# Two decoder layers on one core: the sample group's value products in one PSUM bank with one set of transposes, and the gate's transposes and products in pairs at separate places

## The chip, the cores and the metric

The kernel runs on one core of a Trainium2 chip. The metric is the device time of one execution in microseconds (us), taken as the median of several runs. TensorE is called PE in the profile (PEld is its weight load), VectorE DVE, ScalarE ACT, GpSimd POOL, and SyncE, which issues most transfers, SP.

## The reference, cut to what matters

The program is one inference step of a two-layer decoder. A prompt group of 256 positions and a sample group of 8 sequences, with one new position each and 256 cached ones, share all weights. What the change touches are two things.

The first is the attention of the eight samples over their cached pages, in both layers. A sequence has two pages of 128 positions, 8 heads and 64 columns per head:

```python
# layer 0, softmax; layer 1 has stick-breaking weights in place of p
s = jnp.einsum('hqd,hqjsd->hqjs', qh, ks).astype(jnp.float32) * scale
p = jax.nn.softmax(s.reshape(H, qb, -1), axis=-1).reshape(s.shape)
return jnp.einsum('hqjs,hqjsd->qhd', p.astype(vs.dtype), vs)
```

The second is the spatial gate of layer 0, where each of four groups of 128 channels is mixed over the 128 positions of a chunk by a lower triangular matrix:

```python
w = jnp.tril(sgu_w[:, :c, :c])
vg = v.reshape(B, nc, c, B_GROUPS, B_GROUP_DIM)
f = jnp.einsum('gts,bnsgd->bntgd', w, vg) + sgu_b[:, :c].T[None, None, :, :, None]
return u * f.reshape(B, T, B_WIDTH)
```

## The kernel before

**Layout.** All activations stand transposed: 128 channels of a group on the partitions, the 264 positions (256 of the prompt, then the 8 samples) in the free dimension. So one product with a 128x128 block of weights serves both groups at once.

**Blocks and phases.** `run` (L310) walks through a fixed list of weight blocks per phase: in0, out0, ff0, dn0 for layer 0, and in1, out1, ff1, dn1 for layer 1. A block is three products of 128x264 in one PSUM bank (L329 to L333): high half of the weights by high and by low half of the activations, then low half by high half. Weights come in chunks, are split by ACT (high half, `wh`, L300) and DVE (low half, `wl`, L303) three tiles of eight blocks ahead, in buffers that PE has to free first. in0 has 160 blocks, in1 128; eight blocks in turn make one output `mm`, which DVE then takes out of PSUM. In out0 and out1 the first blocks take `catB` (the gate's or pool mixer's half) in the order of its four parts: block 0 takes part 0, block 2 part 2, block 3 part 3.

**What is put between the blocks.** Everything else that PE does is put between blocks by hand: `blk(b, f)` calls `f` once `b` blocks of the phase have been issued. PE executes in the order written. The times of the calls are the hooks, L925 to L967 for layer 0 and L1126 to L1152 for layer 1.

**PSUM.** Eight banks of 512 fp32 columns: four belong to the pool of `mm` (L228), four to the pool of `at` (L229). `mmb` (L251) borrows a bank from the first pool for other work. A bank is taken again once its reader is done.

**The samples' values.** `sm_tr` (L819) and `zs_tr` (L1066) transpose the weights of all eight sequences, and `to_pz` (L485) copies them into `PZ`, a buffer zeroed once, with 32 columns per page and sequence of which the first eight hold the heads: one ACT instruction per page. `sample_av` (L491) is called for two groups of four sequences: sixteen fp32 products' worth of `pv` into a bank of its own, each sequence in a strip of 32 partitions, then one ACT copy (L498) into `msk`. The calls stand at blocks 157 and 159 of in0 (L957) and 100 and 108 of in1 (L1143). `sample_out` (L503) transposes `msk` back in four 128x128 parts per group, that is eight `po` transposes, and hands out four views, which DVE adds or copies into `osam` (L837, L1076). It is called by `sm_out` at block 4 of out0 and by `zs_out` at block 1 of out1.

**The gate.** `gm_tr(t)` (L887) transposes part t of the normalised `bv` in two 128x128 pieces into a bank `vtp_sgu` of the `mm` pool, and ACT copies it into `vgt` (L522). All four stand at block 150 (L950). `gm_gate(t)` (L896) makes two fp32 products into a bank `pf` of the `mm` pool; DVE adds the bias (L900), multiplies by `bu` (L902), and ACT and DVE make `catB`'s high and low half (L445, L446). All four stand at block 155 (L953). At block 155 of in0 GpSimd also does `gm_own` on the sample columns.

**Stick-breaking around hook 100 of in1.** `z_qk(t)` scores two heads (`Z`, blocks 80, 93, 105, 117); ACT and DVE turn them into weights `w` (sigmoids L1019 and L1020, scan L1021, product L1022); `z_tr(t)` transposes these in 2 x 3 pieces `pt` (blocks 91, 104, 116, and one in out1).

Of the kernel before, what the change touches and what calls it, by code (L numbers as in the profile page):

```python
# [13 lines left out]
AF = mybir.ActivationFunctionType  # L14
# [4 lines left out]
P = 128  # L19
# [3 lines left out]
NS = 8  # L23
T = SEQ + NS
HD = 64
NH = 8
PAST = 256
PAGE = 128
NPG = PAST // PAGE
# [173 lines left out]
def tile_decoder_step(ctx: ExitStack, tc: tile.TileContext, a):  # L203
    nc = tc.nc
    v, s, g = nc.vector, nc.scalar, nc.gpsimd
# [14 lines left out]
    pe = TensorE()  # L220
# [10 lines left out]
    def f4(name, shape=(P, 4, T), dt=F32):  # L231
        return up.tile(list(shape), dt, tag="u", name=name)
# [7 lines left out]
    def at(name):  # L240
        return psa.tile([P, 512], F32, tag="at", name=name)
# [9 lines left out]
    def mmb(name):  # L251

        return psm.tile([P, 512], F32, tag="mm", name=name)
# [5 lines left out]
    def cst(n):  # L259
        o, w = _CST[n]  # L260
        return CST[:, o:o + w]
# [123 lines left out]
    ident = cst("ident")  # L385
# [62 lines left out]
    def page_list(cache, name):  # L448

        tiles, todo = [], []  # L450

        def load(i):
            if i % NPG == 0:
                tiles.append(f4(f"{name}_{i}", (P, NPG, 512)))
            late(tiles[i // NPG][:, i % NPG, :], cache[bass.ds(regs[i], 1), :, :].rearrange("o p f -> (o p) f"))

        return tiles, [lambda i=i: load(i) for i in range(NS * NPG)]
# [27 lines left out]
    def to_pz(src, fn):  # L485

        for pg in range(NPG):
            s.activation(PZ[:, pg, :, 0:NH].rearrange("p s (t c) -> p t s c", c=2),
                         src[:, pg * P:(pg + 1) * P].rearrange("p (t x) -> p t x", x=32)[:, :, :2 * NS].rearrange("p t (s c) -> p t s c", c=2), fn)

    def sample_av(msk, pz, vtiles, gr, name):  # L491
        pv = at(f"pv_{name}{gr}")
        for pg in range(NPG):
            for j in range(4):
                sq = 4 * gr + j
                pe.matmul(pv[32 * j:32 * j + 32, :], pz[:, pg, sq, :], vtiles[sq][:, pg, :],
                          start=pg == 0, stop=pg == NPG - 1)
        s.activation(msk[:, gr], pv, AF.Copy)  # L498

    def sample_av_of(st, pz, vtiles, gr, name):  # L500
        return lambda: sample_av(st["msk"], pz, vtiles, gr, name)

    def sample_out(msk, name):  # L503

        out = []
        for gr in range(2):
            po = at(f"po_{name}{gr}")
            for t in range(4):
                pe.transpose(po[:, 126 * t:126 * t + P], msk[:, gr, t * P:(t + 1) * P], ident)
            for c in range(2):  # L510
                out.append((64 * c, 4 * gr, po[64 * c:64 * c + 64, c::32].rearrange("p (t s) -> p t s", s=4)))
        return out

    PZ = con.tile([P, NPG, NS, 32], F32, name="PZ")
    g.memset(PZ, 0.0)
# [2 lines left out]
    def v_pair(vt, src, t, name, bank=None):  # L518
        p = (bank or at)(f"vtp_{name}{t}")
        for kb in range(2):  # L520
            pe.transpose(p[:, kb * P:(kb + 1) * P], src[:, kb * P:(kb + 1) * P], ident)
        s.activation(vt[:, :, t * P:(t + 1) * P], p[:, :2 * P].rearrange("p (b d) -> p b d", b=2), AF.Copy)  # L522
# [226 lines left out]
    vtiles, vload = page_list(a["vp0"], "V0")  # L749
    st0 = {}  # L750
# [68 lines left out]
    def sm_tr():  # L819
        pr = st0["ps"]  # L820
        pP = mmb("pP")
        for pg in range(NPG):
            pe.transpose(pP[:, pg * P:(pg + 1) * P], pr[:, pg * P:(pg + 1) * P], ident)
        to_pz(pP, AF.Copy)
        pO = mmb("pO")
        pe.matmul(pO[:, :4 * NS], cst("hs"), st0["ow"], start=True, stop=True)
        ob = sm.tile([P, 4, NS], F32, tag="ob", name="ob", bufs=1)
        s.activation(ob, pO[:, :4 * NS].rearrange("p (t s) -> p t s", s=NS), AF.Copy)
        st0["ob"] = ob
        st0["msk"] = f4("msk0", (P, 2, 512))  # L830

    def sm_out():
        osam = sm.tile([P, 4, NS], F32, tag="osam", name="osam", bufs=1)
        v.tensor_tensor(osam, st0["ob"], v4[:, :, SEQ:T], ALU.mult)
        for b, q, po in sample_out(st0["msk"], "l0"):
            o = osam[b:b + 64, :, q:q + 4]
            v.tensor_tensor(o, o, po, ALU.add)  # L837
        halves(catA[0][:, :, SEQ:T], catA[1][:, :, SEQ:T], osam)
# [75 lines left out]
    blk = lambda b, f, *x: hk.at(b / 8 - 1, f, *x)  # L914
# [30 lines left out]
    blk(131, gm_gelu)  # L945
    blk(130, gm_norm)
    blk(140, sm_tr)
    blk(144, lambda: nc.sync.dma_start(a["k0"], k4))
    for t in range(4):
        blk(150, gm_tr, t)  # L950
    blk(155, gm_own)
    for t in range(4):
        blk(155, gm_gate, t)  # L953
    for t, b in enumerate((146, 154, 162)):
        if b <= 160:
            blk(b, lambda t=t: v_pair(vt, v4[:, t, :], t, "v0"))
    for i, b in enumerate((157, 159)):  # L957
        blk(b, sample_av_of(st0, PZ, vtiles, i, "l0"))
# [20 lines left out]
    vtiles, vload = page_list(a["vp1"], "V1")  # L979
# [16 lines left out]
    st1 = {}  # L996
# [69 lines left out]
    def zs_tr():  # L1066
        pP = mmb("pP1")
        for pg in range(NPG):
            pe.transpose(pP[:, pg * P:(pg + 1) * P], st1["zs"][:, pg * P:(pg + 1) * P], ident)
        to_pz(pP, AF.Copy)  # L1070
        st1["msk"] = f4("msk1", (P, 2, 512))

    def zs_out():
        osam = sm.tile([P, 4, NS], F32, tag="osam", name="osam1", bufs=1)
        for b, q, po in sample_out(st1["msk"], "l1"):
            v.tensor_copy(osam[b:b + 64, :, q:q + 4], po)  # L1076
        halves(catA[0][:, :, SEQ:T], catA[1][:, :, SEQ:T], osam)
# [47 lines left out]
    blk = lambda b, f, *x: hk.at(b / 8 - 1, f, *x)  # L1125
    blk(14, norm1)  # L1126
    blk(33, pool_sum)
    for n in range(8):
        blk(40 + 8 * n, drip_of(vload, 2))
    blk(72, zs_score)  # L1130
    blk(82, zs_tr)
    for t, b in enumerate((80, 93, 105, 117)):
        blk(b, z_qk, t)
# [6 lines left out]
        blk(b, pool_mix, i)  # L1140
    for t, b in enumerate((110, 118, 126)):
        blk(b, lambda t=t: v_pair(vt, v4[:, t, :], t, "v1", mmb))
    for i, b in enumerate((100, 108)):  # L1143
        blk(b, sample_av_of(st1, PZ, vtiles, i, "l1"))
    run(orders["in1"], pick(xg), in1_evac, hk)
    hk = Hooks()
# [82 lines left out]
```

## Time and profile before

| What | us |
|---|---|
| median of 3 runs (599.3 to 599.55) | 599.43 |
| the profiled execution | 599.23 |
| its span in the trace | 597.2 |
| PE busy in the span | 588.4 |
| DVE busy in the span | 423.4 |
| ACT busy in the span | 342.5 |
| POOL busy in the span | 104.8 |

The profiled execution is 0.20 us below the median; 2.03 us of it lie outside the span. PE is busy nearly all the time, so whatever it does between the blocks of weights is time of the kernel. A timeline row gives an instruction's start and duration (or those of several alike, with their count), and in brackets how long its engine stood idle before it and what ended that. PE's durations overlap: the next product starts before the last one has ended, so its cost is read from the distance between starts.

### The profile page before, as it was taken

To read this page: it belongs to the slowest core of one execution; us is meant where nothing else is said; L and a number is where in the kernel's file an instruction comes from. 1 tells how busy PE (TensorE), PEld (TensorE's weight loads), DVE (VectorE), ACT (ScalarE), POOL (GpSimd) and SP (SyncE) were. 2 spreads that over 40 slices of the span, in tenths; PEclk is the share of its full clock that TensorE was granted. 3 is DMA by queue.
4 is the path that set the end of the run, shared out by engine and by line. 5 is a ranking of instruction groups with operands and counts; after the bars stand their busy time and mean duration, and the time that the engine had idled before them with its cause. 6 is when DMAs were issued, how large, how long until landed. Compare 5 with 4: busy or idle time off the path is not lost.

```text
span 597.2 us, 12397 instructions
## 1 busy us (share of the span) xinstructions
PE 588.4 (99%) x4907; PEld 570.4 (96%) x4907; DVE 423.4 (71%) x739; ACT 342.5 (57%) x600; POOL 104.8 (18%) x99
## 2 busy tenths in 40 slices
PE   9999999999999999999999999999999999999995
PEld 8999879999999999999999879999999999999994
DVE  7999566877777777655659676687777777864442
ACT  7757845676565655644453556567656565564441
POOL 2100003212313232110120000121232323211110
PEclk9999999999999999999999999999999999999998
DMA  8898844545454545895567763554545454555502
GB/s 334 339 399 348 293 158 156 212 147 204 150 205 153 204 151 202 280 373 201 177 224 278 260 207 97 171 211 148 206 149 206 150 204 156 198 175 198 200 1 74
DMA packets 27707, 122.41 MB, mean 205 GB/s; under 512 B 3330, under 2 KB 4482, under 8 KB 16258
## 3 DMA queue, kind: packets, MB, share of 16 engines
q1 hardware_dynamic: 27072, 120.55, 56.2%
q10 hardware_dynamic: 578, 1.07, 0.5%
q8 instruction: 39, 0.64, 0.4%
q14 instruction: 18, 0.15, 0.1%
HBM read 117.65 MB, written 3.96 MB: 204 GB/s over the span
## 4 chain that ended last, share of the span: by engine, by line
PE 97%; DMA 1%; DVE 1%; ACT 0%; DVEq 0%; issue 0%; SPq 0%
PE mm L215 90%; PE pv_l L215 1%; PE sc L215 1%; PE pav L215 1%; PE pt L218 1%; DMA xw<-in_xw 1%; PE S L215 1%; PE Z L215 1%; PE pf L215 0%; DVE y L643 0%; PE pm L215 0%; PE vtp_v L218 0%; PE po_l L218 0%; PE vtp_sgu L218 0%; PE ns_fin L215 0%; DVE wl L666 0%
## 5 line engine op out<-in xcount | busy, mean ns | idle before, releaser
L303 DVE TENSOR_TENSOR wl<-raw,wh 128x1024 fp32r<-128x1024 f32 x179 | 219.6, 1228 | 74.4 <-ACT wh L300 74.3
L300 ACT ACTIVATE wh<-raw 128x1024 fp32r<-128x1024 f32 x179 | 188.3, 1055 | 90.2 <-PE mm L215 83.3
L215 PE MATMUL mm<-xg_f_h,wh 128*128 128x264 f32 x704 | 200.4, 285 | 0.0
L215 PE MATMUL mm<-xg_f_l,wh 128*128 128x264 f32 x704 | 200.1, 284 | 0.0
L215 PE MATMUL mm<-xg_f_h,wl 128*128 128x264 f32 x704 | 198.9, 283 | 0.0
L215 PEld LDWEIGHTS mm<-xg_f_l,wh 128*128 128x128 f32 x704 | 132.4, 188 | 0.0
L215 PEld LDWEIGHTS mm<-xg_f_h,wh 128*128 128x128 f32 x704 | 132.3, 188 | 0.0
L215 PEld LDWEIGHTS mm<-xg_f_h,wl 128*128 128x128 f32 x704 | 132.3, 188 | 0.0
L585 POOL TENSOR_TENSOR wk<-wk 128x264 f32<-128x264 f32 x44 | 66.2, 1506 | 194.3 <-DVE wk L584 169.0
L215 PE MATMUL mm<-a_h,wh 128*128 128x264 f32 x352 | 100.2, 285 | 0.0
L215 PE MATMUL mm<-a_l,wh 128*128 128x264 f32 x352 | 100.0, 284 | 0.0
L215 PE MATMUL mm<-a_h,wl 128*128 128x264 f32 x352 | 99.5, 283 | 0.0
L215 PEld LDWEIGHTS mm<-a_l,wh 128*128 128x128 f32 x352 | 66.2, 188 | 0.0
L215 PEld LDWEIGHTS mm<-a_h,wh 128*128 128x128 f32 x352 | 66.2, 188 | 0.0
L215 PEld LDWEIGHTS mm<-a_h,wl 128*128 128x128 f32 x352 | 66.1, 188 | 0.0
L445 ACT ACTIVATE a_h<-wk 128x264 fp32r<-128x264 f32 x44 | 18.7, 424 | 73.4 <-POOL wk L585 73.4
L446 DVE TENSOR_TENSOR a_l<-wk,a_h 128x264 fp32r<-128x264 f32 x44 | 19.2, 437 | 41.5 <-ACT a_h L445 41.5
L215 PE MATMUL mm<-xg_h,wh 128*128 128x264 f32 x160 | 47.8, 299 | 0.0
L215 PE MATMUL mm<-xg_h,wl 128*128 128x264 f32 x160 | 45.5, 285 | 0.2 <-DVE wl L666 0.2
L215 PE MATMUL mm<-xg_l,wh 128*128 128x264 f32 x160 | 45.5, 285 | 0.0
L215 PE MATMUL mm<-xg_n_h,wh 128*128 128x264 f32 x128 | 38.5, 301 | 0.0
L215 PE MATMUL mm<-xg_n_l,wh 128*128 128x264 f32 x128 | 36.3, 284 | 0.0
(254 smaller groups left out, 897.7 us busy)
## 6 DMA issues: line engine op xcount, KB each, us to landing
raw<-in_w SPq DMA_DIRECT2D x89, 1024.0 KB, 4.8
K<-in_kt SPq DMA_DIRECT2D x32, 256.0 KB, 6.4
V<-in_vp SPq DMA_DIRECT2D x32, 256.0 KB, 6.9
raw<-in_w SPq DMA_DIRECT2D x4, 512.0 KB, 6.1
X<-in_x SPq DMA_DIRECT2D x4, 264.0 KB, 7.7
xw<-in_xw SPq DMA_DIRECT2D x2, 388.0 KB, 5.4
out_k<-k SPq DMA_DIRECT2D x1, 528.0 KB
out_v<-v SPq DMA_DIRECT2D x1, 528.0 KB, 4.7
```

Of the source, the lines that this page charges most:

```text
L215: return self.keep(nc.tensor.matmul(*x, **k))
L218: return self.keep(nc.tensor.transpose(*x, **k))
L300: i = s.activation(h, src, AF.Copy)
L303: i = v.tensor_tensor(l, src, h.bitcast(F32), ALU.subtract)
L445: s.activation(h, src, AF.Copy)
L446: v.tensor_tensor(l, src, h.bitcast(F32), ALU.subtract)
L585: g.tensor_tensor(A, A, C, ALU.mult)
```

## The change

There are three edits.

1. `to_pz` writes the heads of the second group of sequences into columns 8 to 15 instead of 0 to 7, with one ACT instruction per page and group (four instead of two). `sample_av` makes the products of both groups into one bank `pv`: the second call adds to what the first has left, and a product of one group adds zeros to the rows of the other. The ACT copy into `msk` is made once, after the second call, and `msk` has half the columns. `sample_out` makes four transposes instead of eight; its four views come from one bank. The number of `pv` products stays.
2. The gate's transposes stand at blocks 149, 149, 151 and 151 instead of four times 150; its products at 155, 155, 158 and 158 instead of four times 155. So the second pair of products is issued between the two calls of `sample_av`.
3. In layer 1 `sample_av` stands at blocks 109 and 112 instead of 100 and 108.

```diff
@@ to_pz, sample_av, sample_out
         for pg in range(NPG):
-            s.activation(PZ[:, pg, :, 0:NH].rearrange("p s (t c) -> p t s c", c=2),
-                         src[:, pg * P:(pg + 1) * P].rearrange("p (t x) -> p t x", x=32)[:, :, :2 * NS].rearrange("p t (s c) -> p t s c", c=2), fn)
-
-    def sample_av(msk, pz, vtiles, gr, name):
-        pv = at(f"pv_{name}{gr}")
+            w = src[:, pg * P:(pg + 1) * P].rearrange("p (t x) -> p t x", x=32)[:, :, :2 * NS].rearrange("p t (s c) -> p t s c", c=2)
+            for gr in range(2):
+                s.activation(PZ[:, pg, 4 * gr:4 * gr + 4, gr * NH:gr * NH + NH].rearrange("p s (t c) -> p t s c", c=2), w[:, :, 4 * gr:4 * gr + 4, :], fn)
+
+    def sample_av(st, pz, vtiles, gr, name):
+
+        if gr == 0:
+            st["pv"] = at(f"pv_{name}")
+        pv = st["pv"]
         for pg in range(NPG):
             for j in range(4):
                 sq = 4 * gr + j
                 pe.matmul(pv[32 * j:32 * j + 32, :], pz[:, pg, sq, :], vtiles[sq][:, pg, :],
-                          start=pg == 0, stop=pg == NPG - 1)
-        s.activation(msk[:, gr], pv, AF.Copy)
+                          start=gr == 0 and pg == 0, stop=gr == 1 and pg == NPG - 1, skip_group_check=True)
+        if gr == 1:
+            s.activation(st["msk"], pv, AF.Copy)
 
     def sample_out(msk, name):
 
-        out = []
-        for gr in range(2):
-            po = at(f"po_{name}{gr}")
-            for t in range(4):
-                pe.transpose(po[:, 126 * t:126 * t + P], msk[:, gr, t * P:(t + 1) * P], ident)
-            for c in range(2):
-                out.append((64 * c, 4 * gr, po[64 * c:64 * c + 64, c::32].rearrange("p (t s) -> p t s", s=4)))
-        return out
+        po = at(f"po_{name}")
+        for t in range(4):
+            pe.transpose(po[:, 126 * t:126 * t + P], msk[:, t * P:(t + 1) * P], ident)
+        return [(64 * c, 4 * gr, po[64 * c:64 * c + 64, 8 * gr + c::32].rearrange("p (t s) -> p t s", s=4)) for gr in range(2) for c in range(2)]
@@ layer 0
-        st0["msk"] = f4("msk0", (P, 2, 512))
+        st0["msk"] = f4("msk0", (P, 512))
     for t in range(4):
-        blk(150, gm_tr, t)
+        blk((149, 149, 151, 151)[t], gm_tr, t)
     blk(155, gm_own)
     for t in range(4):
-        blk(155, gm_gate, t)
+        blk((155, 155, 158, 158)[t], gm_gate, t)
@@ layer 1
-        st1["msk"] = f4("msk1", (P, 2, 512))
+        st1["msk"] = f4("msk1", (P, 512))
-    for i, b in enumerate((100, 108)):
+    for i, b in enumerate((109, 112)):
         blk(b, sample_av_of(st1, PZ, vtiles, i, "l1"))
```

More of the change, by code (lines that the diff above doesn't have):

```diff
@@ L496, in sample_av @@
                 pe.matmul(pv[32 * j:32 * j + 32, :], pz[:, pg, sq, :], vtiles[sq][:, pg, :],
-                          start=pg == 0, stop=pg == NPG - 1)
-        s.activation(msk[:, gr], pv, AF.Copy)
+                          start=gr == 0 and pg == 0, stop=gr == 1 and pg == NPG - 1, skip_group_check=True)
+        if gr == 1:
+            s.activation(st["msk"], pv, AF.Copy)
     def sample_av_of(st, pz, vtiles, gr, name):
-        return lambda: sample_av(st["msk"], pz, vtiles, gr, name)
+        return lambda: sample_av(st, pz, vtiles, gr, name)
     def sample_out(msk, name):
-        out = []
-        for gr in range(2):
-            po = at(f"po_{name}{gr}")
-            for t in range(4):
-                pe.transpose(po[:, 126 * t:126 * t + P], msk[:, gr, t * P:(t + 1) * P], ident)
-            for c in range(2):
-                out.append((64 * c, 4 * gr, po[64 * c:64 * c + 64, c::32].rearrange("p (t s) -> p t s", s=4)))
-        return out
+        po = at(f"po_{name}")
+        for t in range(4):
+            pe.transpose(po[:, 126 * t:126 * t + P], msk[:, t * P:(t + 1) * P], ident)
+        return [(64 * c, 4 * gr, po[64 * c:64 * c + 64, 8 * gr + c::32].rearrange("p (t s) -> p t s", s=4)) for gr in range(2) for c in range(2)]
     PZ = con.tile([P, NPG, NS, 32], F32, name="PZ")
```

## The prediction

> **What bounds the kernel now.** I read the page first: busy times, then the chain of work that ended last.
>
> ```profile
> PE 588.4 (99%) x4907; PEld 570.4 (96%) x4907; DVE 423.4 (71%) x739; ACT 342.5 (57%) x600; POOL 104.8 (18%) x99
> PE 97%; DMA 1%; DVE 1%; ACT 0%; DVEq 0%; issue 0%; SPq 0%
> ```
>
> PE is 97% of the chain. So a microsecond that PE doesn't spend between the blocks of weights is one off the time, and what only ACT, DVE or a transfer does counts only where PE would come to wait for it. The next view is PE's timeline where foreign work is put in, because PE's durations overlap and only distances between starts tell a cost.
>
> ```profile
> 72.24 0.28 PE L215 MATMUL mm<-xg_l,wh 128*128 128x264 f32 x1
> 72.36 0.28 PE L215 MATMUL mm<-xg_h,wl 128*128 128x264 f32 x1
> 72.49 0.38 PE L218 MATMUL vtp_v<-CST,v 128*128 128x128 f32 x2
> 72.62 0.37 PE L215 MATMUL mm<-xg_h,wh 128*128 128x264 f32 x1
> 72.83 0.29 PE L215 MATMUL mm<-xg_l,wh 128*128 128x264 f32 x1
> ```
>
> Undisturbed, products start 0.12 us apart (72.24, 72.36), a block of three takes 0.36. The measure that I use throughout is: start of the second product after the insertion, minus start of the last before it, minus the 0.24 that two steps take anyway. Here it gives 72.83 - 72.36 - 0.24 = 0.23 us for two transposes.
>
> **The `po` transposes, halved in both layers.** The eight of layer 0 in the same timeline:
>
> ```profile
> 87.09 0.28 PE L215 MATMUL mm<-catB_h,wl 128*128 128x264 f32 x1
> 87.22 1.03 PE L218 MATMUL po_l<-CST,msk 128*128 128x128 f32 x8
> 88.01 0.37 PE L215 MATMUL mm<-catB_h,wh 128*128 128x264 f32 x1
> 88.21 0.28 PE L215 MATMUL mm<-catB_l,wh 128*128 128x264 f32 x1
> ```
>
> 88.21 - 87.09 - 0.24 = 0.88. From two to eight the cost grows by 0.65, 0.108 per transpose, and at two it is already almost nothing but that: an insertion of transposes has next to no fixed price. Four, which have no row, lie between 0.23 and 0.88; the line through both ends gives 0.45. Saved: 0.43 per layer, **0.86** for two.
>
> **The gate's transposes in two pairs.** Before, all four `vtp_sgu` (eight transposes) stand together:
>
> ```profile
> 74.05 0.28 PE L215 MATMUL mm<-xg_h,wl 128*128 128x264 f32 x1
> 74.17 1.30 PE L218 MATMUL vtp_sgu<-CST,bv 128*128 128x128 f32 x8
> 74.59 1.30 ACT L522 ACTIVATE vgt<-vtp_sgu 128x256 f32<-128x256 f32 x4 [0.34 <-PE vtp_sgu L218]
> 75.03 0.20 PEld L218 LDWEIGHTS vtp_sgu<-CST,bv 128*128 128x128 f32 x2 [0.28 <-ACT vgt L522]
> 75.22 0.37 PE L215 MATMUL mm<-xg_h,wh 128*128 128x264 f32 x1
> ...
> 75.43 0.28 PE L215 MATMUL mm<-xg_l,wh 128*128 128x264 f32 x1
> ```
>
> They cost 75.43 - 74.05 - 0.24 = 1.14, where eight `po` cost 0.88. The row at 75.03 says why: of the four `mm` banks the running output holds one, so the fourth pair waits for ACT's first copy. Two insertions of four cost 2 x 0.45 = 0.90. Saved: **0.24**, if the second pair finds its bank free.
>
> **The gate's products in two pairs.** Sixteen records (each fp32 product leaves two):
>
> ```profile
> 77.23 0.28 PE L215 MATMUL mm<-xg_h,wl 128*128 128x264 f32 x1
> 77.23 1.43 PEld L215 LDWEIGHTS pf<-sguc,vgt 128*128 128x128 f32 x12
> ...
> 78.83 0.52 PEld L215 LDWEIGHTS pf<-sguc,vgt 128*128 128x128 f32 x4 [0.17 <-DVE bv L900]
> ...
> 79.50 0.28 PE L215 MATMUL mm<-xg_l,wh 128*128 128x264 f32 x1
> ```
>
> Cost: 79.50 - 77.23 - 0.24 = 2.03. The first twelve loads take 1.43, the last of them 0.19 itself, so they come 0.113 apart; the twelfth starts at 78.47, the thirteenth at 78.83 instead of 78.58, because its bank had to be read by DVE first. That is 0.25 of standing. Eight records have no row: without a fixed price they cost 8 x 0.113 = 0.90, two insertions 1.80, and 0.23 is saved. The other end is that a separate insertion costs as much again as the standing, which saves nothing. I take **0.23**, since the nearest row, the two transposes in the same 128*128 shape, shows no fixed price.
>
> **The `pv` products.** Their number stays. In layer 1 they move:
>
> ```profile
> 349.97 0.28 PE L215 MATMUL mm<-xg_n_h,wl 128*128 128x264 f32 x1
> 350.18 1.92 PE L215 MATMUL pv_l<-V,PZ 128*32 128x512 f32 x16
> 352.03 0.39 PE L215 MATMUL mm<-xg_n_h,wh 128*128 128x264 f32 x1
> 352.26 0.28 PE L215 MATMUL mm<-xg_n_l,wh 128*128 128x264 f32 x1
> ```
>
> A call costs 352.26 - 349.97 - 0.24 = 2.05 wherever it stands. Half of its products add to an open bank already (the second page), so adding in the second call is nothing new. Cost: 0.
>
> **What becomes late.** With the call at hook 100 gone, PE comes to the transposes of hook 104 earlier: 349.97 plus four blocks (1.45) is 351.42. The second three of them, 0.33 later at 351.75, need the stick-breaking product of the fourth head:
>
> ```profile
> 350.90 0.55 DVE L1022 TENSOR_TENSOR w<-w,keep 128x384 f32<-128x384 f32 x1
> ```
>
> It is done at 351.45, and all that it hangs on lies ahead of hook 100, so it doesn't move. 0.3 us remain, a call's 2.05 less than before. After that, PE's work until hook 116 is the same in sum, and DVE and ACT are only earlier. Cost 0.
>
> In layer 0 the late gate pair stands after hook 158 and `catB`'s part 3 is wanted by the fourth block of out0:
>
> ```profile
> 81.74 1.01 DVE L446 TENSOR_TENSOR catB_l<-bu,catB_h 128x264 fp32r<-128x264 f32 x2
> ...
> 85.31 0.29 PE L215 MATMUL mm<-catB_h,wh 128*128 128x264 f32 x1
> ...
> 86.77 0.37 PE L215 MATMUL mm<-catB_h,wh 128*128 128x264 f32 x1
> ```
>
> Before, 86.77 against 82.75. After, PE is 0.47 earlier (the two gate terms): out0 starts at 84.84, part 3 is wanted at 86.30. Back from 84.84, a block, a call of `pv`, a block and the pair itself put its start at 84.84 - 0.36 - 2.05 - 0.36 - 0.90 = 81.17 and its end near 82.2. Then bias, two products with `bu`, high half and low half follow, five steps on DVE and ACT over at most 264 columns, none longer than the 0.55 us of the product over 384 in the row above: 82.2 + 2.75 = 84.95 at most. 1.35 us remain.
>
> The copy into `msk` comes once instead of twice, and PE doesn't wait for it:
>
> ```profile
> L498 ACT ACTIVATE msk<-pv_l 128x512 f32<-128x512 f32 x4 | 2.4, 598 | 5.6 <-PE pv_l L215 5.6
> L488 ACT ACTIVATE PZ<-pP 128x64 f32<-128x64 f32 x4 | 0.7, 256 | 0.0
> ```
>
> ACT waits for PE there (5.6 us), so the two copies less are worth nothing. The two `PZ` instructions more per layer stand ahead of other work of ACT:
>
> ```profile
> 71.87 0.32 ACT L488 ACTIVATE PZ<-pP 128x64 f32<-128x64 f32 x2
> ...
> 73.84 0.41 ACT L522 ACTIVATE vt<-vtp_v 128x256 f32<-128x256 f32 x1
> ```
>
> Two take 0.32 together at 0.256 each, so one more costs ACT between 0.06 and 0.26, two more 0.12 to 0.51; I take 0.2. The copy `vt` then ends at 74.25 + 0.2 = 74.45, the first `vgt` copy starts there, and PE gets its bank 0.44 after that start (74.59 to 75.03 before): 74.89. The second pair of transposes starts at 74.05 - 0.36 + 0.45 + 0.73 = 74.87, its second half, which takes that bank, at 75.08. It fits by 0.19; at 0.51 PE would stand 0.12. By the Trainium skill (ScalarE: Activation LUTs, section Rules for kernel authors), an ACTIVATE takes about 0.3 us plus 0.83 ns per element, so two more of 32 elements would be 0.65 us. By that estimate PE would stand 0.26 us, the pairing of the transposes would gain nothing, and the sum would be 1.33 - 0.24 = 1.09; the two rows above speak for less, and no run here shows the four.
>
> **The sum.** 0.86 + 0.24 + 0.23 = 1.33 us. Against the profiled execution, 599.23 - 1.33 = 597.90; that execution lies 0.20 below the median, so against 599.43 it gives **598.1**, 0.22% less. A measurement of this kernel can tell about 0.2%, 1.2 us, from no change: the forecast is just beyond that, at 598.23.
>
> **Rivals.**
>
> *The pairs gain nothing* (0.16): ACT is late with the copies ahead of the second pair, as bounded above, and each insertion of products has a price of its own. For it: the 0.19 of room is small. Against it: two transposes at 0.23. Only the `po` term stays: 599.43 - 0.86 = 598.57, within 0.2%. ACT alone at its dear end gives 598.10 + 0.12 = 598.22. By the figure of the Trainium skill's page it would be 599.43 - 1.09 = 598.34.
>
> *The cover at hook 100 was needed* (0.08).
>
> ```profile
> L303 DVE TENSOR_TENSOR wl<-raw,wh 128x1024 fp32r<-128x1024 f32 x179 | 219.6, 1228 | 74.4 <-ACT wh L300 74.3
> ```
>
> A low half of weights, 1.23 us on DVE, comes ahead of the stick-breaking product at 350.90; PE stands 1.23 - 0.30 = 0.93 at hook 104, and the time is 599.0. Against it: in the changed kernel's order of instructions that low half still stands behind.
>
> *Adding to an open bank is dear* (0.05, slower): the second call adds in all of its four rounds of four strips, eight rounds over both layers. Four rounds fill the 1.92 of a call, 0.48 each at most; were a round of adds to take as much again, 8 x 0.48 = 3.8 us would come on top: 601.9. From 0.17 per round the gain is gone, from 0.32 it is slower by over 0.2%. Against it: two of the four rounds in that row, those of the second page, add already.
>
> *It doesn't do what it says* (0.02): were the transposes not fewer, only the 0.47 of the pairs would stay, 598.96. The order of instructions shows four `po` per layer, so this is all but excluded.
>
> **How the numbers follow.** The forecast has 0.66, and 0.03 are left for something better. The runs before spread by 0.25 us, so of the forecast's 0.66 some 0.07 lie on the near side of 598.23: faster 0.62, slower 0.05, the rest 0.33. The range goes from 597.7 (the spread, and up to 0.15 of standing that I have not seen) to 598.9, which takes in the first rival with the spread; the other three, 0.15, stay out in the main.
>
> **What would show it.** In the changed profile, four `po` cost near 0.45 in each layer; two insertions of `vtp_sgu` near 0.45 and two of `pf` near 0.90 stand without a wait of PEld for ACT or DVE; the `pt` of hook 104 cost 6 x 0.108 = 0.65 with no wait for L1022; out0 starts without one for L445 or L446; a `pv` call still costs 2.05. I am wrong if one of these waits, or if a half insertion of `pf` costs over 1.0.

## The result, and the profile after

| Kernel | median, us | runs | before beside it, us | ratio, 95% interval |
|---|---|---|---|---|
| changed | 597.92 (597.5 to 598.98) | 16 | 599.31 (598.93 to 599.55, 16 runs) | 0.9979 [0.9972, 0.9986] |

By the ratio the change takes 0.21% off; between the two medians lie 1.39 us. 598.1 us was forecast, a gain of 1.33 us. The ratio's interval stands for 0.84 to 1.68 us, which holds that gain but also the 0.86 of the first rival, so the terms have to be read from the profile. The profiled execution took 598.02 us with a span of 596.0 us, against 599.23 and 597.2. The lines of its page that answer to those shown of before are the busy times and the chain's shares by engine:

```profile
PE 587.2 (99%) x4899; PEld 569.4 (96%) x4899; DVE 422.8 (71%) x739; ACT 340.9 (57%) x602; POOL 105.1 (18%) x99
PE 97%; DMA 1%; DVE 1%; ACT 0%; DVEq 0%; issue 0%; SPq 0%
```

PE still is the chain. It has eight records fewer (4907 to 4899): the four `po` saved in each layer. Its busy time fell by 1.2 us, as much as the span. Now the same insertions as in the prediction, with the same measure (start of the second product behind, minus start of the last one ahead, minus 0.24). The gate's transposes, timeline of the changed kernel over PE, PEld and ACT:

```profile
73.87 0.28 PE L215 MATMUL mm<-xg_h,wl 128*128 128x264 f32 x1
73.89 0.47 PEld L218 LDWEIGHTS vtp_sgu<-CST,bv 128*128 128x128 f32 x4
...
74.41 0.70 ACT L523 ACTIVATE vgt<-vtp_sgu 128x256 f32<-128x256 f32 x2
...
74.56 0.28 PE L215 MATMUL mm<-xg_l,wh 128*128 128x264 f32 x1
...
75.04 0.28 PE L215 MATMUL mm<-xg_h,wl 128*128 128x264 f32 x1
75.05 0.47 PEld L218 LDWEIGHTS vtp_sgu<-CST,bv 128*128 128x128 f32 x4
...
75.73 0.28 PE L215 MATMUL mm<-xg_l,wh 128*128 128x264 f32 x1
```

Each pair costs 0.45 (74.56 - 73.87 - 0.24 and 75.73 - 75.04 - 0.24). PEld makes all four loads of the second pair in one row, with no bracket for ACT; before, the last two stood 0.28 for `vgt`. The gate's products with a `pv` call between them, PE alone:

```profile
77.16 0.28 PE L215 MATMUL mm<-xg_h,wl 128*128 128x264 f32 x1
77.28 1.06 PE L215 MATMUL pf<-sguc,vgt 128*128 128x128 f32 x8
...
78.30 0.28 PE L215 MATMUL mm<-xg_l,wh 128*128 128x264 f32 x1
...
78.79 0.28 PE L215 MATMUL mm<-xg_h,wl 128*128 128x264 f32 x1
79.00 1.92 PE L215 MATMUL pv_l<-V,PZ 128*32 128x512 f32 x16
...
81.08 0.28 PE L215 MATMUL mm<-xg_l,wh 128*128 128x264 f32 x1
81.20 0.28 PE L215 MATMUL mm<-xg_h,wl 128*128 128x264 f32 x1
81.33 1.05 PE L215 MATMUL pf<-sguc,vgt 128*128 128x128 f32 x8
...
82.34 0.28 PE L215 MATMUL mm<-xg_l,wh 128*128 128x264 f32 x1
```

Eight records of `pf` cost 78.30 - 77.16 - 0.24 = 0.90, and again 0.90 at 81.20; the `pv` call between them costs 81.08 - 78.79 - 0.24 = 2.05, as before. Layer 0's four `po`, and the place in layer 1 where the cover was taken away (`pt` at block 104, `Z` at 105):

```profile
86.79 0.28 PE L215 MATMUL mm<-catB_h,wl 128*128 128x264 f32 x1
86.92 0.60 PE L218 MATMUL po_l<-CST,msk 128*128 128x128 f32 x4
...
87.47 0.28 PE L215 MATMUL mm<-catB_l,wh 128*128 128x264 f32 x1
```

```profile
350.68 0.28 PE L215 MATMUL mm<-xg_n_h,wl 128*128 128x264 f32 x1
350.80 0.82 PE L218 MATMUL pt<-CST,w 128*128 128x128 f32 x6
...
351.58 0.28 PE L215 MATMUL mm<-xg_n_l,wh 128*128 128x264 f32 x1
351.70 0.29 PE L215 MATMUL mm<-xg_n_h,wl 128*128 128x264 f32 x1
351.92 0.93 PE L215 MATMUL Z<-k4b,q4b 64*128 64x128 f32 x8
...
353.00 0.28 PE L215 MATMUL mm<-xg_n_l,wh 128*128 128x264 f32 x1
```

`po` 0.44, `pt` 0.66 without a wait, `Z` 1.06. By insertions the change gives:

| What | before | after | gain |
|---|---|---|---|
| `po`, two layers | 0.88 + 0.88 | 0.44 + 0.44 | 0.88 |
| gate transposes | 1.14 | 0.44 + 0.45 | 0.25 |
| gate products | 2.03 | 0.90 + 0.90 | 0.23 |
| `pv`, four calls | 4 x 2.05 | 4 x 2.05 | 0 |
| sum | | | 1.36 |

The profiled execution is 1.21 us shorter, not 1.36: in it PE was late by 0.19 before the change begins. The product ahead of block 146's `vtp_v` starts at 72.55 where before it started at 72.36, and what PE does ahead of that is the same work in both. With it the two agree within 0.04.

### The profile page after: what moved, and what is told of

Same layout as the page of the kernel before. It is cut to its first block, busy times and chain, and to the rows that moved or that the text cites. A ratio compares the mean times of both kernels' runs of the same rounds, so it can differ in the third digit from the quotient of the medians.

```text
span 596.0 us, 12377 instructions
## 1 busy us (share of the span) xinstructions
PE 587.2 (99%) x4899; PEld 569.4 (96%) x4899; DVE 422.8 (71%) x739; ACT 340.9 (57%) x602; POOL 105.1 (18%) x99
## 4 chain that ended last, share of the span: by engine, by line
PE 97%; DMA 1%; DVE 1%; ACT 0%; DVEq 0%; issue 0%; SPq 0%
PE mm L215 90%; PE pv_l L215 1%; PE sc L215 1%; PE pav L215 1%; PE pt L218 1%; DMA xw<-in_xw 1%; PE S L215 1%; PE Z L215 1%; DVE y L644 0%; PE pf L215 0%; PE pm L215 0%; PE vtp_v L218 0%; PE po_l L218 0%; PE vtp_sgu L218 0%; PE ns_fin L215 0%; DVE wl L667 0%
```

## The experiments

Theory: PE's insertions between the blocks are the time; the pairs save the standing for a fourth bank, `po` saves by its number, and the move in layer 1 is neutral. Rivals stand at each run. All are edits of the changed kernel. Before ran beside them, at a median of 599.48 (the first four), 599.50 (the next three) and 599.54 us (the last three). Many medians lie closer together than their intervals are wide, so the insertions in the profile decide between theories.

| Run | median, us | ratio to before, 95% interval | profiled, us |
|---|---|---|---|
| gate together | 598.46 | 0.9980 [0.9971, 0.9989] | 598.49 |
| move undone | 598.41 | 0.9982 [0.9973, 0.9991] | 598.41 |
| three and one | 598.02 | 0.9979 [0.9970, 0.9988] | 597.85 |
| calls joined | 597.61 | 0.9967 [0.9955, 0.9979] | 597.30 |
| sixteen copies | 598.39 | 0.9983 [0.9973, 0.9992] | 598.04 |
| bank from `mm` | 597.91 | 0.9975 [0.9963, 0.9988] | 597.90 |
| calls split | 599.28 | 0.9998 [0.9989, 1.0007] | 599.28 |
| full array | 617.04, one run | | 617.04 |
| joined at 100 | 597.35 | 0.9956 [0.9943, 0.9970] | 597.35 |
| changed, again | 598.40 | 0.9974 [0.9963, 0.9985] | 598.49 |

### The gate's work together again

```diff
-        blk((149, 149, 151, 151)[t], gm_tr, t)
+        blk(150, gm_tr, t)
-        blk((155, 155, 158, 158)[t], gm_gate, t)
+        blk(155, gm_gate, t)
```

> The changed kernel with edit 2 undone: all four gate transposes at block 150 and all four gate products at 155, as before. Theory (the pairs save the standing for a fourth bank): one insertion of `vtp_sgu` costs 1.14 again and one of `pf` 2.03, with PEld waiting 0.3 us for ACT's `vgt` and 0.2 for DVE's `bv`; against the changed kernel, whose two insertions each cost 0.44 + 0.45 and 0.90 + 0.90, that is 0.25 + 0.23 = 0.48 us more, 598.4. Rival (the pairs gain because the work stands elsewhere, not because of the bank): the insertions cost the same 0.89 and 1.79 together and the time stays at 597.9.

Measured: `vtp_sgu` 1.14, `pf` 2.03, 0.48 more than the pairs, and 598.46. The list of PEld's waits has both rows again that the changed kernel's list lacks (columns: total us, times, longest):

```profile
PEld vtp_sgu L218 <- ACT vgt L523: 0.3, 1, 0.3
PEld pf L215 <- DVE bv L901: 0.2, 1, 0.2
```

The two waits together are the gain of edit 2. This run brings back the old places and the old grouping at once, so by itself it doesn't exclude the rival, that the place alone gains. The run with three parts and one, below, does: at the old places, 150 and 155, three parts cost 0.66 and 1.35, and PEld's list has neither wait.

### The move in layer 1 undone

```diff
-    for i, b in enumerate((109, 112)):
+    for i, b in enumerate((100, 108)):
```

> The changed kernel with edit 3 undone: in layer 1 the two calls of the value products at blocks 100 and 108 again, now with one bank open between them. Theory A, that of the prediction (the move is neutral): each call costs 2.05, `Z` at block 105 1.06, `pt` at 104 0.66, the time is that of the changed kernel, 597.9. Theory B (the open bank is missing elsewhere): `Z` at block 105 takes two of the four banks of the `at` pool, with one held open and one still being read by ACT's copy of `pt` it has to stand; its insertion costs 1.3 to 2.0 instead of 1.06, and the time is 0.3 to 0.9 us longer, up to 598.8.

Measured: 598.41. `pv` 2.05, `pt` 0.66, but `Z` at block 105 costs 1.51 instead of 1.06. Timeline of this run over PE, then PEld, then ACT around block 105:

```profile
353.59 0.29 PE L215 MATMUL mm<-xg_n_h,wl 128*128 128x264 f32 x1
353.81 1.37 PE L215 MATMUL Z<-k4b,q4b 64*128 64x128 f32 x8
...
355.34 0.28 PE L215 MATMUL mm<-xg_n_l,wh 128*128 128x264 f32 x1
```

```profile
353.80 0.29 PEld L215 LDWEIGHTS Z<-k4b,q4b 64*128 64x128 f32 x2
354.26 0.52 PEld L215 LDWEIGHTS Z<-k4b,q4b 64*128 64x128 f32 x6 [0.16 <-ACT pT L1053]
```

```profile
353.73 0.85 ACT L1053 ACTIVATE pT<-pt 128x384 f32<-128x384 f32 x2
```

`Z` begins, loads for its first bank, and stands until ACT has copied the first `pt` out of a bank. Theory B holds: the open `pv` bank takes one of four `at` banks from block 100 to 108; the two `pt` of block 104 have two, the first `Z` the last, and the second `Z` has none. So edit 3 isn't free to leave out: without it the change would give 0.45 less.

### The same, with the bank from the other pool

```diff
-            st["pv"] = at(f"pv_{name}")
+            st["pv"] = mmb(f"pv_{name}") if name == "l1" else at(f"pv_{name}")
-    for i, b in enumerate((109, 112)):
+    for i, b in enumerate((100, 108)):
```

> The calls of the value products in layer 1 at blocks 100 and 108 again, as in the run with edit 3 undone, but their bank is taken from the pool of `mm` instead of the pool of `at`. Theory (in that run `Z` at block 105 stood 0.45 us only for lack of a fourth `at` bank): the insertion of `Z` costs 1.06 again, and as `mm` needs one running bank and one that DVE reads, three left there do for the rest; the time is that of the changed kernel, 597.9. Rival (`Z` stands because of the order of the work, whatever the bank): it costs 1.5 again, 598.4. A third outcome: the `mm` outputs or `vtp_v` lack the bank now, and a wait of `mm` for DVE shows instead.

Measured: 597.91, and at block 105 in PE's timeline:

```profile
353.53 0.29 PE L215 MATMUL mm<-xg_n_h,wl 128*128 128x264 f32 x1
353.75 0.93 PE L215 MATMUL Z<-k4b,q4b 64*128 64x128 f32 x8
...
354.83 0.28 PE L215 MATMUL mm<-xg_n_l,wh 128*128 128x264 f32 x1
```

354.83 - 353.53 - 0.24 = 1.06. Same blocks, another pool, no standing: it was the bank. Behind the first 8 us of the program the list has no wait of `mm` for another engine, and none of `vtp_v`, so the third outcome did not come either.

### Three parts and one

```diff
-        blk((149, 149, 151, 151)[t], gm_tr, t)
+        blk((150, 150, 150, 151)[t], gm_tr, t)
-        blk((155, 155, 158, 158)[t], gm_gate, t)
+        blk((155, 155, 155, 158)[t], gm_gate, t)
```

> The changed kernel with the gate's parts as three and one instead of two and two: transposes at 150, 150, 150, 151 and products at 155, 155, 155, 158. Theory (only the fourth part in a row lacks a bank, and transposes and products have no price per insertion): six transposes cost 6 x 0.11 = 0.66 and two 0.22, twelve records of `pf` 1.35 and four 0.45, together 2.68 as in pairs (2.68), the time is 597.9. Rival (a long row costs by its length, or an insertion by itself): three in a row stand already and cost 0.1 to 0.3 us more, or the last single one costs more than its share.

Measured: `vtp_sgu` 0.66 + 0.22, `pf` 1.35 + 0.45, together 2.68; 598.02. For records of 128 columns in shape 128*128 the cost is their number times 0.11, at two, four, six, eight and twelve records, whatever their grouping, where none waits for a bank. Only the fourth part in a row stands. The rival falls.

### Sixteen copies into `PZ`

```diff
-            for gr in range(2):
-                s.activation(PZ[:, pg, 4 * gr:4 * gr + 4, gr * NH:gr * NH + NH].rearrange("p s (t c) -> p t s c", c=2), w[:, :, 4 * gr:4 * gr + 4, :], fn)
+            for sq in range(NS):
+                c0 = sq // 4 * NH
+                s.activation(PZ[:, pg, sq:sq + 1, c0:c0 + NH].rearrange("p s (t c) -> p t s c", c=2), w[:, :, sq:sq + 1, :], fn)
```

> The changed kernel with `PZ` filled by sixteen ACT instructions per layer (one per page and sequence) instead of four. In the changed kernel's trace the four start 0.077 us apart (72.056 to 72.283). Theory (ACT pays 0.08 to 0.1 per small copy, and the second pair of `vtp_sgu` has 0.4 us of room): twelve more put the first `vgt` copy 0.9 to 1.2 us later, past the room by 0.5 to 0.8, so the insertion of the second pair costs 0.95 to 1.25 instead of 0.445, with PEld waiting for ACT's `vgt`; layer 1 has nothing of PE waiting on these copies; the time is 598.4 to 598.7. Rival (each copy costs what one takes by itself, 0.18 to 0.2 us): 2.3 us later, the pair stands 1.9 and the time is 599.8. By the Trainium skill (ScalarE: Activation LUTs, section Rules for kernel authors), about 0.3 us each, the pair would stand 3.2 us or more, an estimate from that page.

Measured: the second pair costs 0.77 instead of 0.445, a standing of 0.33, less than either theory. ACT's timeline, first of the changed kernel, then of this run:

```profile
72.06 0.44 ACT L490 ACTIVATE PZ<-pP 128x32 f32<-128x32 f32 x4
72.36 0.22 ACT L829 ACTIVATE ob<-pO 128x32 f32<-128x32 f32 x1
...
74.13 0.43 ACT L523 ACTIVATE vt<-vtp_v 128x256 f32<-128x256 f32 x1
```

```profile
71.79 1.20 ACT L491 ACTIVATE PZ<-pP 128x8 f32<-128x8 f32 x16
72.71 0.37 ACT L830 ACTIVATE ob<-pO 128x32 f32<-128x32 f32 x1
...
74.47 0.58 ACT L524 ACTIVATE vt<-vtp_v 128x256 f32<-128x256 f32 x1
```

From the first copy to the next instruction, `ob`, four copies take 72.36 - 72.06 = 0.30 and sixteen, of the same number of elements in all, 72.71 - 71.79 = 0.92: 0.62 for twelve more, 0.05 each. `vt` shows the same. This run lies 0.27 ahead (71.79 against 72.06), so `vt` is 74.47 + 0.27 - 74.13 = 0.61 later. The theory's 0.08 to 0.1 was too dear, and the rival's 0.18 to 0.2 is excluded. PE stands for 0.33 of that, so the room was about 0.28. PEld's list has the wait for ACT's `vgt` again, 0.3 us.

The Trainium skill (ScalarE: Activation LUTs, section Rules for kernel authors) budgets about 0.3 us per ACTIVATE whose bias is an operand; an estimate from it for twelve is 3.6. The trace has a sixth of that. These copies have no bias operand, and their distance in a row isn't what one takes by itself, so the figure doesn't fit this case. The time (598.39) tells nothing by itself, since a copy of the changed kernel later measured 598.40.

### The calls joined

```diff
-    for i, b in enumerate((157, 159)):
+    for i, b in enumerate((159, 159)):
-    for i, b in enumerate((109, 112)):
+    for i, b in enumerate((112, 112)):
```

> The changed kernel with the two calls of the value products joined at one block in each layer: both at 159 in in0, both at 112 in in1. Theory (a call has a fixed price): a call costs 2.05, and its sixteen records fill four rounds in which the rounds start about 0.43 us apart, so about 0.33 of the 2.05 are spent at its two ends, where the products of 128*128 and those of 128*32 meet; joined, 32 records cost 2 x 2.05 - 0.33 = 3.77 instead of 4.11, and two layers give 0.66 us: 597.3. Rival 1 (no fixed price, the ends are only the usual overlap): 4.1 together, the time stays at 597.9. Rival 2 (a row of 32 brings PE's next weights or the sequencer out of step, or the copy into `msk` comes late for the transposes after block 4 of out0): a wait of 0.2 to 0.5 us, so 597.9 to 598.4. The Trainium skill (TensorEngine Tiling (Array Packing), section Key Properties) says that a change of the tiling mode drains TensorE, without a figure; by it the joined calls gain, by an amount that it leaves open.

Measured: 597.61; the joined insertions cost 3.77 and 3.77 instead of twice 2.05 each. In layer 1, PE's timeline:

```profile
355.05 0.28 PE L215 MATMUL mm<-xg_n_h,wl 128*128 128x264 f32 x1
355.26 3.64 PE L215 MATMUL pv_l<-V,PZ 128*32 128x512 f32 x32
358.83 0.39 PE L215 MATMUL mm<-xg_n_h,wh 128*128 128x264 f32 x1
359.05 0.28 PE L215 MATMUL mm<-xg_n_l,wh 128*128 128x264 f32 x1
```

359.05 - 355.05 - 0.24 = 3.76 by the rounded starts. So a call has a fixed price of 0.33 to 0.34 (2 x 2.05 - 3.77 = 0.33, and 0.34 with the starts unrounded). 0.09 of it stand ahead of the first record, which starts 0.21 behind the stream's last product instead of 0.12 (355.05 to 355.26). The rest can't be read from one distance: the 0.22 between the two products behind (358.83 to 359.05) are hardly more than the 0.20 behind the eight `po` of before (88.01 to 88.21), which had no fixed price. Rival 1 falls; of rival 2 there is no wait in the profile.

### The calls split

```diff
-        for pg in range(NPG):
-            for j in range(4):
+        gr, pg = i // 2, i % 2
+        for j in range(4):
...
-                          start=gr == 0 and pg == 0, stop=gr == 1 and pg == NPG - 1, skip_group_check=True)
-        if gr == 1:
+                      start=i == 0, stop=i == 3, skip_group_check=True)
+        if i == 3:
...
-    for i, b in enumerate((157, 159)):
+    for i, b in enumerate((156, 157, 158, 159)):
...
-    for i, b in enumerate((109, 112)):
+    for i, b in enumerate((109, 110, 111, 112)):
```

> The changed kernel with each call of the value products split into its two pages: four calls per layer, at 156, 157, 158, 159 in in0 and 109, 110, 111, 112 in in1, all into the one bank. Measured so far: sixteen records in one insertion 2.05, thirty-two 3.77. Theory (0.33 per insertion and 0.1075 per record): eight records cost 1.19, four insertions 4.78 instead of 4.11, so 0.67 per layer and 1.34 in all: 599.3, the whole gain of the change lost without a wait anywhere. Rival (what joining saved was a wait or an overlap peculiar to that place): eight records cost half of sixteen, 1.03, and the time stays at 597.9.

Measured: 599.28, as the theory gives. The first of the eight insertions in PE's timeline:

```profile
78.27 0.28 PE L215 MATMUL mm<-xg_h,wl 128*128 128x264 f32 x1
78.48 1.06 PE L215 MATMUL pv_l<-V,PZ 128*32 128x512 f32 x8
...
79.70 0.28 PE L215 MATMUL mm<-xg_l,wh 128*128 128x264 f32 x1
```

79.70 - 78.27 - 0.24 = 1.19. So 8, 16 and 32 records cost 1.19, 2.05 and 3.77: 0.33 and 0.1075 per record. Behind the first 8 us of the program neither PE nor PEld has a new wait for another engine. Among PEld's waits the price shows in one row, that of `mm` that ended without a releaser that the profile shows ("issue"); its three versions, of the changed kernel, of the calls joined and of the calls split:

```profile
PEld mm L215 <- issue: 6.8, 15, 0.8
```

```profile
PEld mm L215 <- issue: 5.1, 13, 0.8
```

```profile
PEld mm L215 <- issue: 10.1, 19, 0.8
```

Two insertions fewer are two such stops fewer, four more are four more. The 0.8 of each isn't its price (the last round still runs meanwhile), but their count is that of the insertions.

### `pv` over the full array

```diff
-                pe.matmul(pv[32 * j:32 * j + 32, :], pz[:, pg, sq, :], vtiles[sq][:, pg, :],
-                          start=gr == 0 and pg == 0, stop=gr == 1 and pg == NPG - 1, skip_group_check=True)
+                pe.matmul(pv, pz[:, pg, 4 * gr:4 * gr + 4, :].rearrange("p s c -> p (s c)"), vtiles[sq][:, pg, :],
+                          start=gr == 0 and pg == 0 and j == 0, stop=gr == 1 and pg == NPG - 1 and j == 3, skip_group_check=True)
...
-    for i, b in enumerate((157, 159)):
+    for i, b in enumerate((159, 159)):
```

> What the 0.33 per insertion of `pv` hangs on. As the changed kernel, but each `pv` product takes the 128 columns of `PZ` of all four sequences of its group (128*128 like the products of `mm`) instead of 32 (128*32) and writes the whole bank, so that the sums of the sequences run together (that part of the computation is changed); in layer 0 the two calls are joined at block 159, in layer 1 they stand apart at 109 and 112. The four strips no longer run side by side, so a call takes longer: sixteen records of 512 columns, by the 0.12 of 264 columns between 0.23 and 0.43 each. Theory (the price is that of going from 128*128 to 128*32 and back): the joined insertion costs just twice a single one, and a single one is sixteen times the distance of its records, within 0.1. Rival (the price is that of long products or of the change of operands): 0.3 less for the joined pair again. By the Trainium skill (TensorEngine Tiling (Array Packing), section Key Properties) it is the change of tiling mode that drains TensorE, which agrees with the theory.

PE's timeline, the joined insertion of layer 0 and the first single one of layer 1:

```profile
80.08 0.28 PE L215 MATMUL mm<-xg_h,wl 128*128 128x264 f32 x1
80.20 13.90 PE L215 MATMUL pv_l<-V,PZ 128*128 128x512 f32 x32
...
94.06 0.28 PE L215 MATMUL mm<-xg_l,wh 128*128 128x264 f32 x1
```

```profile
363.52 0.28 PE L215 MATMUL mm<-xg_n_h,wl 128*128 128x264 f32 x1
363.65 7.03 PE L215 MATMUL pv_l<-V,PZ 128*128 128x512 f32 x16
...
370.64 0.28 PE L215 MATMUL mm<-xg_n_l,wh 128*128 128x264 f32 x1
```

13.74 joined against 6.88 single: joining saves 0.02 at most. The records start 0.429 apart, and 16 x 0.429 is 6.87, so nothing is left for a fixed price. The first record starts 0.12 to 0.13 behind the stream's last product, no longer 0.21. The tensors, the 512 columns that stream through and the number of records are the same, so the 0.33 aren't the price of long products or of foreign operands: they belong to going from 128*128 to 128*32 and back. Two things differ there, though, the shape of the array and four strips that run side by side, and no run separates them. Products in other shapes start as late: `Z` (64*128) 0.22 behind the stream, 351.70 to 351.92 in the changed kernel, and the attention's `pav` (128*64) 0.21, 88.67 to 88.88. The Trainium skill (TensorEngine Tiling (Array Packing), section Key Properties) says that a change of the tiling mode drains TensorE. The trace fits that, with 0.33 us for the way there and back, but shows no drain as such.

### Joined at block 100, and the changed kernel again

```diff
-    for i, b in enumerate((157, 159)):
+    for i, b in enumerate((159, 159)):
-    for i, b in enumerate((109, 112)):
+    for i, b in enumerate((100, 100)):
```

> The calls of the value products joined, at 159 in layer 0 as in the run with joined calls, but at block 100 in layer 1 instead of 112. Theory (the bank was short only because it was open from 100 to 108): joined, it is open for 3.8 us only, ACT has read it before block 104, `Z` at 105 costs 1.06, `pt` at 104 0.66, and the time is that of the run with the calls joined at 112, 597.3 to 597.6. Rival (block 105 stands whenever a call lies ahead of it): `Z` costs 1.5, the time is 0.45 longer.

> The changed kernel itself, unchanged, for a comparison on the same chip with the joined calls: 597.9, and 0.68 above the joined calls at 100 if the two savings of 0.34 are all that joining does.

Measured: joined 597.35, the changed kernel 598.40 beside it. `pv` 3.77 in each layer, `Z` at 105 1.06, `pt` at 104 0.66: with the calls joined no bank stays open, and edit 3's place doesn't matter. Of the 1.05 between the two medians the insertions explain 0.68. In the two profiles 0.35 more lie ahead of anything that differs: the product ahead of the first gate transposes starts at 73.87 in the one and 74.22 in the other. So joined calls, at either place, are 0.68 us below the changed kernel by their insertions. By time this isn't shown: joined at 100 is 0.9956 [0.9943, 0.9970] of before, and the interval overlaps that of the changed kernel beside it (0.9963 to 0.9985).

## Why the prediction was right, point by point

- **The time**: forecast 1.33 off 599.43, measured 1.36 by insertions. Before stood at 599.31 beside the changed kernel, not 599.43, so 0.12 of the distance between 598.1 and 597.92 is the base's.
- **`po`**: forecast 0.86, measured 0.88. Four transposes lie on the line between two and eight, and so do six `vtp_sgu` (0.66) in the run with three and one.
- **Gate transposes**: forecast 0.24, measured 0.25. That the fourth bank was the cause is shown by the run with the gate together and the one with three parts and one.
- **Gate products**: forecast 0.23, measured 0.23. That an insertion of `pf` has no price of its own, the choice between 0 and 0.23, is shown by 0.90, 1.35 and 0.45 at eight, twelve and four records.
- **ACT's two copies more**: taken at 0.2, room 0.19. They cost 0.10 (from the first copy to `vt` 74.13 - 72.06 = 2.07, before 73.84 - 71.87 = 1.97), and by the run with sixteen copies the room behind that was about 0.28. The first rival was further off than it looked. The rival time of 598.34 was worked out from the Trainium skill (ScalarE: Activation LUTs, section Rules for kernel authors), whose figure is for an ACTIVATE with a bias operand; these copies have none.
- **Layer 1's move at nothing**: right, but the reason was not the whole one. The prediction asked whether work became late when the cover went (`pt` did not stand: the product that it needs ended at 350.71, 0.42 ahead, where 0.3 had been forecast), and didn't ask what the old place would have cost. An open bank at blocks 100 to 108 makes `Z` stand 0.45, so the move is what makes the first edit pay in full in layer 1.
- **`pv` unchanged at 2.05**: right, and taken as one piece. That 0.33 of it is a price per insertion was not seen, nor that the change, which joined the bank, left the two calls apart. It lay open in the rows: sixteen records that fill four rounds of 0.43 make 1.72, not 2.05.
- **`catB`**: the changed kernel ended part 3 at 84.45 (two rows of `catB_l` from 83.67, 0.78 in all), and block 3 of out0 began at 86.46. 2.0 us of room; at least 1.35 had been forecast.
- **Adding to an open bank** (the rival on the other side): each second call still costs 2.05, though all its rounds add. It falls.

## What to carry to other kernels

Where PE is the chain, count the insertions between its products by the distance between starts, and ask of each whether its cost is its number of records (here 0.11 each for 128 columns in the stream's own shape, free to be split) or has a price per insertion (0.33 for `pv`, where the shape changes), and join only the second kind. A bank kept open across calls is missing to whatever stands between them: count the banks at every block from the first call to the last. With gains of a few tenths, compare insertions in the profile rather than medians, since what lies ahead of the change, the same work in both, left PE 0.35 us apart in two executions.

## What the runs showed of the hardware that was not expected

- Going from 128*128 to 128*32 products and back costs 0.33 us, the same at 8, 16 and 32 records, and nothing when products of the same width run in 128*128. `Z`, in 64*128, and `pav`, in 128*64, start as late behind the stream (0.21 to 0.22); whether they carry the same price wasn't tried.
- Small ACT copies that don't depend on each other start close together: two of 64 elements 0.10 us apart (before, 71.87 to `ob` at 72.08), four of 32 0.075, sixteen of 8 0.058, though the groups list each of these last with 0.285 on the mean (32 in both layers).
- Four `pv` products of 32 columns run side by side (a round of four each 0.43), where a single one over 128 columns takes the same 0.43: the strips are worth a factor of four by the round and of 3.4 by the call, whose ends are paid too (2.05 against 6.88).
